# Decoder trunk: the first two unit pairs of each up projection go product by product, with their weights split during the projection before

## The chip, the core and the metric

One core of a Trainium2 chip runs the whole kernel. The metric is the device time in microseconds, as the median of several runs. PE is TensorE, DVE is VectorE, ACT is ScalarE, SP is the engine whose queue issues most DMAs.

## What is computed

The reference is a decoder trunk of two layers on x of 1024 tokens by 1024 features, float32. Layer 0 mixes by sparse attention beside a short gated convolution, layer 1 by a recurrent block (RG-LRU). Each layer ends with a gated convolution FFN, which is where the change lies:

```python
def rmsnorm(x, g):
    y = x * rsqrt(mean(x * x) + 1e-6)
    return y * g
def conv_ffn(h, w_up, conv_w, conv_b, w_down):
    u = causal_dwconv(h @ w_up, conv_w, conv_b)
    return (silu(u[..., :D_FF]) * u[..., D_FF:]) @ w_down
x = x + mixer(rmsnorm(x, norm_mix))
x = x + conv_ffn(rmsnorm(x, norm_ffn), ...)
```

D_FF is 2816, so `w_up` is 1024 by 5632 and `w_down` 2816 by 1024.

## The kernel before, in words

**Precision.** Every matmul of weights is made of three: operands are split into a high part (ACT copies the float32 to fp32r) and a low part (DVE subtracts the high part from the original), and `mm3` (L139) adds high by high, high by low, low by high. `split` (L145) is this pair of operations, so each weight tile and each activation tile costs one ACT and one DVE operation before PE may use it.

**The residual** X lies in SBUF as 8 feature chunks by 2 token halves, tiles of 128x512. While an FFN's up projection runs, X is in DRAM (`xd`): each finished half chunk is stored from ACT's queue (`ProductNorm.add`) and loaded again before the down projection.

**The up projection** (`up_pairs`, L312) uses a seven-product scheme for 2x2 blocks (Strassen in Winograd's form) in place of eight. Channels are taken in 22 pairs of units, a gate unit and an up unit of 128 channels each. A pair is seven products, named 1 to 7; a product is 12 matmuls of 128x512 into a PSUM bank. The left operands are halves of weight tiles or of their sums (`wA` for products 1 and 2, `w4` for 4, `sums` then `wG` for 6 and 3, `wU` for 7 and 5). The right operands are seven "pages" of four tiles each, high and low: the normalised X chunks and their differences. Pages 1 and 2 need the first token half alone. Page 5 needs scaled chunks of the second half, page 3 is the second half itself, 6 and 7 are differences, and 4 builds on 6. The banks: 1, 6, 7, 4 add up in bank A, 5 and 3 in bank Bk, 2 is in C; copies and additions between them (`c1`, `c2`, copies to `zu`, `zg`) yield the unit's z tiles, which `post` convolves (one ACT and two DVE operations of 1024 columns for each of two units), gates and stores to `fd` in DRAM.

**The order.** Everything in `up_pairs` is inside `in_order` (L95), which ties each instruction to the one before it on its engine, so PE, DVE, ACT and SP each run this stage in exactly the order of the text. Outside such a block a list scheduler orders each engine's instructions, with earlier program text first. The block begins

```python
wA(0), w4(0), sums(0), wG(0), wU(0), wA(1)
load(2)
p1(0), c1(0), p2(0), p1(1), c1(1), p2(1)
```

and then takes each pair as 5, 6, (1 of the next), 7, 3, (2 of the next), 4.

**The entry to an FFN.** `ProductNorm` collects the squares of X: ACT squares a chunk, DVE adds it to a running sum, and `rstd` multiplies by a matrix of ones on PE (`ss`, L1339, full float32), then ACT takes Ln and Exp to get R. For the first token half `done` does this and makes pages 1 and 2. For the second half `finish` (called at the start of `ffn`, outside the in-order block) does it and makes the pages 5, 6, 7, 3, 4 in turn, all before the block in program order. In layer 0 the entry is the end of `even_layer`: X's two halves are loaded from `yd`, the first half is squared and stored to `xd` again, and the rest of the attention's output projection (four tiles `W`, 24 matmuls each) is added to the second half. In layer 1 it is `down_last` (L269) of the recurrent block: four tiles `D` of 12 matmuls each and each token half, and `done` for the first half after the third tile of the second half.

**The turn to the down projection.** After the block the main pools are opened again, X is loaded, the y tiles (`yr` from `fd`, four channels for the first group) are split into pages, and `down` (L254) multiplies group by group into PSUM tiles `D` (four buffers of two banks), which `accum` adds to X.

Of the kernel before, what the change touches and what calls it, by code (L numbers as in the profile page):

```python
# [18 lines left out]
FP = mybir.dt.float32  # L19
# [40 lines left out]
class Kern:  # L60
# [60 lines left out]
    def split_w(self, raw, n=1024, pool_lo=False, parts=1):  # L121
        nc = self.nc
        self.nw += 1
        W, b = (self.W2, 1) if self.W2 is not None and self.nw % 3 == 0 else (self.W, 2)
        hi = W.tile([P, 1024], FR, tag="wh", bufs=b, name=self.nm("wh"))
        lo = W.tile([P, 1024], FR, tag="wl", bufs=b, name=self.nm("wl"))
# [5 lines left out]
        return hi, lo  # L132

# [120 lines left out]
    def down(self, wsrc, ng, ys, bias=None):  # L254
        nf = 8 // ng
        for ft in range(8 // nf):
            w = self.load_w(wsrc(ft))
# [11 lines left out]
    def down_last(self, wsrc, ng, ys, fin):  # L269
        nf = 8 // ng  # L270
        ws_ = [self.load_w(wsrc(ft)) for ft in range(8 // nf)]
        prev = None
        for sl in fin.slices:
# [4 lines left out]
            for f0 in range(0, 8, 2):  # L278
# [19 lines left out]
    def pages(self, p, xn):  # L298
        hi, lo = (self.page(p) for _ in range(2))
        return self.split(hi, lo, xn)  # L300

    def page(self, p):
        pool, bufs = (self.Bp, 24) if p in "374" else (self.Ap, 32)
        return pool.tile([P, HT], FR, tag="h", bufs=bufs, name=self.nm("h"))
# [7 lines left out]
    def up_pairs(self, srcs, B, post):  # L312

        nc = self.nc
        n = len(srcs)
        act, v = nc.scalar.activation, nc.vector.tensor_tensor
        raw, wt, st = {}, {}, {}
        at = lambda w, h: [x[:, half_of(h)] for x in w]  # L320
        bank = lambda: self.Q.tile([P, HT], FP, tag="q", bufs=8, name=self.nm("q"))
        z = lambda: self.cp.tile([P, S], FP, tag="c", bufs=6, name=self.nm("z"))

        def load(i):
            if i < n:
                raw[i] = [self.load_raw(srcs[i][0])]
                raw[i].append(self.W3.tile([P, S], FP, tag="wr", bufs=2, name=self.nm("wr")))
                nc.sync.dma_start(raw[i][1], srcs[i][1])

        def hi_lo(pool, n, tag, bufs, x):  # L330
            t = lambda c: pool.tile([P, n], FR, tag=tag + c, bufs=bufs, name=self.nm(tag + c))
            return self.split(t("h"), t("l"), x)
# [1162 lines left out]
```

## Time and profile before

| | us |
|---|---|
| runs: median (lowest, highest) | 2444.49 (2443.89, 2446.0) |
| the profiled execution | 2452.43 |
| its span, first to last instruction | 2449.8 |
| PE busy | 2275.6 (93%) |
| DVE busy | 1699.5 (69%) |
| ACT busy | 1166.2 (48%) |

Mean granted clock of TensorE: 0.961. All rows come from the one profiled execution; they are read as shares and differences, which are then set against the median of the runs. A row of the timeline gives the start, the length, the operation and in brackets the idle time of the engine before it with what ended it. Matmuls overlap, so the spacing of starts is what a matmul costs, not its length. `L141`, `L142` and `L143` are the three matmuls of `mm3`, so products are told apart by their operands (`q<-h,wh`: 1 and 2; `q<-h,sh`: 5, 6, 7, 3; `q<-h,ah`: 4).

### The profile page before, as it was taken

Reading aid. Unit: us, or ns where it says so; the run is one execution under the profiler, and the core shown is the slowest. Engines: PE = TensorE matmul, PEld = TensorE weight load, DVE = VectorE, ACT = ScalarE, POOL = GpSimd, SP = SyncE. Lnnn points to the kernel's source line nnn. Section 1 sums busy time; section 2 is a strip of 40 time slices with the busy share of each in tenths; the row PEclk is TensorE's granted clock in tenths of the full one; section 3 lists DMA queues with packets and bytes.
Section 4 is the critical chain, followed back from the end, with each engine's and each line's share of the span. In section 5 each row is a group of like instructions: output and inputs, shape, how many; then the busy total and the mean of one; then the engine's idle time right before and its main releaser. Section 6 shows DMA issues by size and latency. Waiting matters only on the chain.

```text
span 2449.8 us, 26485 instructions
## 1 busy us (share of the span) xinstructions
PE 2275.6 (93%) x10162; PEld 1842.5 (75%) x10162; DVE 1699.5 (69%) x2448; ACT 1166.2 (48%) x1699; POOL 170.2 (7%) x123
## 2 busy tenths in 40 slices
PE   7899999999659999999999999998599999999997
PEld 5788777777438888887888777886488888878886
DVE  6456778988687777777534657768787777765346
ACT  5652666766444444444212365575344444432114
POOL 4002233221000000000000210000000000000001
PEclk9899999999879999999999999999799999999998
DMA  4113112222421222222513111112122222243221
GB/s 140 57 54 117 52 52 69 91 78 83 159 86 69 78 89 92 78 78 101 208 52 104 45 48 56 44 49 103 35 78 78 81 95 83 73 176 129 78 78 69
DMA packets 71327, 207.27 MB, mean 85 GB/s; under 512 B 7969, under 2 KB 11553, under 8 KB 71073
## 3 DMA queue, kind: packets, MB, share of 16 engines
q1 hardware_dynamic: 65088, 193.79, 23.2%
q10 hardware_dynamic: 5472, 9.71, 1.0%
q0 software_dynamic: 640, 2.10, 0.2%
q8 instruction: 79, 1.29, 0.2%
q14 instruction: 48, 0.39, 0.0%
HBM read 161.52 MB, written 44.04 MB: 84 GB/s over the span
## 4 chain that ended last, share of the span: by engine, by line
PE 71%; DVE 10%; ACT 4%; issue 2%; DMA 1%; POOL 0%; DVEq 0%; ACTq 0%; SPq 0%; POOLq 0%
PE q L143 12%; PE q L141 11%; PE q L142 11%; PE D L142 7%; PE D L143 7%; PE D L141 7%; PE U L143 2%; PE U L142 2%; PE U L141 2%; PE T L939 2%; PE O L922 2%; DVE h L147 1%; PE F L141 1%; PE F L142 1%; PE F L143 1%
## 5 line engine op out<-in xcount | busy, mean ns | idle before, releaser
L130 ACT ACTIVATE wh<-wr 128x1024 fp32r<-128x1024 f32 x120 | 127.0, 1058 | 392.8 <-PE D L142 274.1
L141 PE MATMUL q<-h,sh 128*128 128x512 f32 x704 | 277.2, 394 | 2.7 <-ACT z L396 2.7
L142 PE MATMUL q<-h,sh 128*128 128x512 f32 x704 | 277.1, 394 | 0.0
L143 PE MATMUL q<-h,sl 128*128 128x512 f32 x704 | 277.1, 394 | 0.0
L250 DVE TENSOR_TENSOR x<-D,x 128x512 f32<-128x512 f32 x192 | 123.8, 685 | 205.7 <-PE D L143 203.9
L244 DVE SCALAR_TENSOR_TENSOR c<-z,par,c 128x1023 f32<-128x1023 f32 (+1 forms) x176 | 225.2, 1280 | 12.3 <-ACT c L242 9.2
L141 PE MATMUL U<-hh,wh 128*128 128x512 f32 x480 | 191.2, 399 | 12.7 <-ACT wh L130 12.7
L142 PE MATMUL U<-hl,wh 128*128 128x512 f32 x480 | 191.3, 399 | 7.2 <-DVE hl L195 7.1
L143 PE MATMUL U<-hh,wl 128*128 128x512 f32 x480 | 190.2, 397 | 2.2 <-DVE wl L131 2.2
L141 PE MATMUL q<-h,wh 128*128 128x512 f32 x352 | 143.3, 407 | 48.1 <-ACT wh L146 48.1
L141 PE MATMUL D<-y,wh 128*128 128x512 f32 (+1 forms) x464 | 180.9, 391 | 0.0
L143 PE MATMUL D<-y,wl 128*128 128x512 f32 (+1 forms) x464 | 180.8, 390 | 0.0
L142 PE MATMUL D<-y,wh 128*128 128x512 f32 (+1 forms) x464 | 180.8, 390 | 0.0
L141 PEld LDWEIGHTS q<-h,sh 128*128 128x128 f32 x704 | 132.2, 188 | 34.4 <-ACT z L396 4.4
L142 PEld LDWEIGHTS q<-h,sh 128*128 128x128 f32 x704 | 132.3, 188 | 30.5
L143 PEld LDWEIGHTS q<-h,sl 128*128 128x128 f32 x704 | 132.4, 188 | 30.3
L242 ACT ACTIVATE c<-z,par 128x1024 f32<-128x1024 f32 x88 | 109.2, 1240 | 89.8 <-DVE z L406 89.7
L143 PE MATMUL q<-h,wl 128*128 128x512 f32 x352 | 141.0, 401 | 2.6 <-DVE wl L147 2.6
L142 PE MATMUL q<-h,wh 128*128 128x512 f32 x352 | 140.5, 399 | 0.0
L131 DVE TENSOR_TENSOR wl<-wr,wh 128x1024 fp32r<-128x1024 f32 x96 | 120.5, 1257 | 26.7 <-ACT wh L130 23.5
L147 DVE TENSOR_TENSOR sl<-wr,sh 128x1024 fp32r<-128x1024 f32 x88 | 107.6, 1225 | 43.4 <-ACT sh L146 43.4
L146 ACT ACTIVATE sh<-wr 128x1024 fp32r<-128x1024 f32 x88 | 92.6, 1055 | 85.3 <-PE q L142 80.5
(310 smaller groups left out, 5292.7 us busy)
## 6 DMA issues: line engine op xcount, KB each, us to landing
wr<-in_wup SPq DMA_DIRECT2D x88, 512.0 KB, 4.3
fd<-c SPq DMA_DIRECT2D x44, 512.0 KB, 2.9
yr<-fd SPq DMA_DIRECT2D x44, 512.0 KB, 4.2
wr<-in_wd SPq DMA_DIRECT2D x40, 512.0 KB, 3.7
wr<-in_wbc SPq DMA_DIRECT2D x24, 512.0 KB, 3.5
xd<-x ACTq DMA_DIRECT2D x32, 256.0 KB, 2.1
x<-xd SPq DMA_DIRECT2D x32, 256.0 KB, 6.1
wr<-in_cin SPq DMA_DIRECT2D x16, 512.0 KB, 3.6
```

The lines of the kernel that those rows point to most:

```text
L130: nc.scalar.activation(hi[:, s], raw[:, s], AF.Copy)
L131: eng.tensor_tensor(lo[:, s], raw[:, s], hi[:, s].bitcast(FP), op=OP.subtract)
L141: mm(out, whi, xhi, start=first, stop=False, skip_group_check=resumed)
L142: mm(out, whi, xlo, start=False, stop=False, skip_group_check=resumed)
L143: mm(out, wlo, xhi, start=False, stop=last, skip_group_check=resumed)
L146: self.nc.scalar.activation(hi, t, AF.Copy)
L147: (eng or self.nc.vector).tensor_tensor(lo, t, hi.bitcast(FP), op=OP.subtract)
L242: nc.scalar.activation(o, src, AF.Identity, bias=b, scale=w(K - 1))
L244: nc.vector.scalar_tensor_tensor(o[:, s:], src[:, :n - s], w(K - 1 - s), o[:, s:], op0=OP.mult, op1=OP.add)
L250: nc.vector.tensor_tensor(x, ps, x, op=OP.add)
L922: nc.tensor.matmul(O, vv, hl[k], start=False, stop=last and k == 1)
L939: nc.tensor.transpose(T[:, hh * P:hh * P + P], cur["P"][:, hh, kb * P:kb * P + P], self.ident)
```

## The change

A class `Up` takes the place of `up_pairs`, with the order inside a steady pair the same but for `post`, whose first step moves behind the next pair's `w4` and whose last (the multiply and the store to `fd`) comes before `wA` of the next but one.

- **Weights early.** `fin.weights()` (`Up.prologue`) stands in `down_last` and in the attention's output projection after its second tile. It loads the weights of pairs 0 and 1, splits for both the halves of products 1, 2 and 4 (512 columns each) and makes the weight sums, in pools of their own.
- **Products as pages come.** `lead`, all of it in the in-order block, takes both pairs together: products 1, 2; page 5, products 5; page 3, products 3; page 6, products 6; page 7, products 7; page 4, products 4; the half weights of each product are split just behind its page. Product 1 of pair 2 follows, then the rest of the preparation for pairs 2 and 3 and the gating of pair 0.
- **The sums of squares** of the second half are no longer added on DVE: the eight squares are multiplied by ones on PE one by one into `ss` (eight matmuls of full float32 in place of one), six of them inside the projection. The first half keeps its sum on DVE; its `done` now comes after the first tile of the second half (layer 1, `late = 0`) or after the second W tile (layer 0), where two of the four W weights are loaded ahead and the first half of X isn't stored, since `yd` holds it.
- **Residual tiles turn into pages.** X's pool stays open with 16 rotating tiles; page 7, the low parts of page 4 and the tiles of `w4` take those whose values are used up.
- **The turn.** Before the last pair, inside the block, the first down weight and the first four y channels are loaded (through the two raw weight buffers) and split. X is loaded chunk by chunk, both halves.

```diff
@@ Kern
-    def down(self, wsrc, ng, ys, bias=None):
+    def down(self, wsrc, ng, ys, bias=None, pre=()):
...
-            w = self.load_w(wsrc(ft))
+            w = pre.pop(0) if pre else self.load_w(wsrc(ft))
...
     def down_last(self, wsrc, ng, ys, fin):
...
         ws_ = [self.load_w(wsrc(ft)) for ft in range(8 // nf)]
+        fin.weights()
...
-                if prev is not None and f0 == 4:
+                if prev is not None and f0 == fin.late:
...
     def ffn(self, l, nm, fin):
...
-            nm.finish()
-            self.main_close()
             self.us.close()
...
+            with self.pool(f"Q{l}", space=PS) as up.Q, self.in_order():
+                up.lead(nm, right)
+                up.steady()
+                cur = [up.y_pages(ci) for ci in range(UP_GROUPS[0][1])]
+                up.finish()
...
+        pre = [up.wd, self.load_w(io["wd"][l, 0, 1])]
+        for f in range(KC):
+            for half in range(2):
+                nc.sync.dma_start(self.X[f][half], self.xd[half][f][:, half_of(half)])
...
@@ even_layer
-        ws = [self.load_w(io["woa"][0, 0])]
+        ws = [self.load_w(io["woa"][0, ft]) for ft in range(2)]
...
-                    fin.add(f, 0, self.X[f][0])
-        fin.done(slice(0, HT))
+                    fin.add(f, 0, self.X[f][0], False)
...
+            if ft < 2:
+                ws.append(self.load_w(io["woa"][0, ft + 2]))
+            if ft == 1:
+                fin.weights()
...
+            if ft == 1:
+                fin.done(slice(0, HT))
...
+class Up:
+    RAW = {"1": (0, 0), "2": (0, 1), "6": (0, 0), "3": (0, 1), "7": (1, 0), "5": (1, 1)}
...
+    def half(self, p, i):
+        r, h = self.RAW[p]
+        self.wt[i, p] = self.hi_lo(self.Wx, HT, "x", 4, self.raw[i][r][:, half_of(h)])
...
+    def prologue(self):
+        k = self.k
+        self.pages()
+        self.Wx = self.xs.enter_context(k.pool(f"Wx{self.l}"))
+        for i in range(2):
+            self.load(i)
+        for p in "12":
+            for i in range(2):
+                self.half(p, i)
+        for i in range(2):
+            self.w4(i)
+        for i in range(2):
+            self.sums(i)
+
+    def lead(self, nm, right):
+        k, two = self.k, (0, 1)
+        nm.rstd1()
+        for i in two:
+            self.p1(i)
+        for i in two:
+            self.p2(i)
+        nm.page5()
+        for i in two:
+            self.half("5", i)
+        for i in two:
+            self.c1(i)
...
+        for i in two:
+            self.mm(i, "5", Bk[i], True)
+        nm.page3()
+        for i in two:
+            self.half("3", i)
+        for i in two:
+            self.act(zu[i][:, HT:], Bk[i])
+        for i in two:
+            self.mm(i, "3", Bk[i], False)
+        nm.page6()
+        for i in two:
+            self.half("6", i)
+        for i in two:
+            self.c2(i)
+        for i in two:
+            self.mm(i, "6", A[i], False)
+        nm.page7()
+        for i in two:
+            self.half("7", i)
+        for i in (2, 3):
+            self.load(i)
+        for i in two:
+            self.act(zg[i][:, HT:], A[i])
+        for i in two:
+            self.mm(i, "7", A[i], False)
+        nm.page4()
+        for i in two:
+            self.v(zg[i][:, HT:], Bk[i], zg[i][:, HT:], OP.add)
+        self.wA(2)
+        for i in two:
+            self.v(zu[i][:, HT:], A[i], zu[i][:, HT:], OP.add)
+        for i in two:
+            self.mm(i, "4", A[i], False)
+        self.p1(2)
...
+        self.w4(2)
+        self.sums(2)
+        self.act(zu[0][:, :HT], A[0])
+        self.wU(2)
+        t = self.post(0, (zg[0], zu[0]))
+        next(t)
+        self.act(zu[1][:, :HT], A[1])
+        self.c1(2)
+        self.p2(2)
+        self.wG(2)
+        self.wA(3)
...
+    def y_pages(self, ci):
+        k = self.k
+        if ci == 0:
+            self.wd = k.load_w(k.io["wd"][self.l, 0, 0])
+        raw = k.load_raw(k.fd[ci])
+        return k.y_halves(raw)
+
+    def finish(self):
+        self.pair(self.n - 1)
+        for _ in self.tail:
+            pass
...
 class ProductNorm:
...
+    late = 0
...
+            t = self.up.sq[f]
+            nc.scalar.activation(t, x, AF.Square)
+            self.t.append(t)
+            if f % 2 and f > 1:
+                self.sums(f - 3)
...
+    def sums(self, f0):
...
+        for f in (f0, f0 + 1):
+            nc.tensor.matmul(self.ss, k.ones, self.t[f], start=f == 0, stop=f == KC - 1)
...
+    def rstd1(self):
+        self.k.ln_exp(self.R[:, HT:], self.ss)
...
+    def page5(self):
+        k, X = self.k, self.k.X
+        self.up.B["5"] = [(k.page(), k.page()) for _ in range(4)]
         for i in range(4):
-            b11, b12 = X[i][0], self.scaled(i, 1)
-            v(b11, b12, b11, op=OP.subtract)
-            B["5"][i] = k.pages("5", b11)
+            self.minus(X[i][0], self.scaled(i, 1), X[i][0])
+            k.split(*self.up.B["5"][i], X[i][0])
...
+    def page7(self):
+        k, X = self.k, self.k.X
         for i in range(4):
-            B["3"][i] = k.pages("3", X[4 + i][1])
-        for i in range(4):
-            b21, t2 = X[4 + i][0], X[i][0]
-            v(b21, b21, t2, op=OP.subtract)
-            B["4"][i] = k.pages("4", b21)
+            self.minus(X[i][1], X[4 + i][1], X[i][1])
+        hi, lo = ([k.x_tile(FR) for _ in range(4)] for _ in range(2))
+        self.up.B["7"] = [k.split(hi[i], lo[i], X[i][1]) for i in range(4)]
```

## Rows read from the trace of the kernel before

**Rows 1.** The page, part 1: busy us, share, instructions.

```profile
PE 2275.6 (93%) x10162; PEld 1842.5 (75%) x10162; DVE 1699.5 (69%) x2448; ACT 1166.2 (48%) x1699; POOL 170.2 (7%) x123
```

**Rows 2.** Waits of PE: us in total, times, longest.

```profile
PE q L141 <- ACT wh L146: 48.1, 2, 25.2
PE ss L1339 <- DVE sq L210: 34.3, 3, 20.1
PE D L141 <- ACT h L146: 7.4, 2, 3.7
PE q L141 <- ACT z L396: 2.7, 4, 0.7
PE D L142 <- DVE h L147: 1.5, 2, 0.8
```

**Rows 3.** Windows: length, busy by engine (PE, PEld, DVE, ACT, POOL), clock, DMA.

```profile
690.00:736.00 46.00, 18.44 (x52) 13.11 (x52) 36.93 (x57) 19.34 (x31) 0.00 (x0) 0.63 0.11 36
...
789.30:1137.18 347.88, 347.88 (x1513) 284.08 (x1512) 273.54 (x289) 166.78 (x199) 0.00 (x0) 1.00 0.23 81
1812.69:2160.57 347.88, 347.88 (x1514) 284.06 (x1512) 273.56 (x289) 166.79 (x199) 0.00 (x0) 1.00 0.23 81
```

**Rows 4.** Timeline of PE, layer 0: start, us, operation, idle before.

```profile
662.76 2.08 PE L1339 MATMUL ss<-sq,ones 128*128 128x512 f32 x2 [20.08 <-DVE sq L210]
...
689.79 0.39 PE L143 MATMUL W<-og,wl 128*128 128x512 f32 x1
693.21 2.07 PE L1339 MATMUL ss<-sq,ones 128*128 128x512 f32 x2 [3.03 <-DVE sq L210]
...
725.59 0.79 PE L141 MATMUL q<-h,wh 128*128 128x512 f32 x1 [22.92 <-ACT wh L146]
...
735.88 0.39 PE L141 MATMUL q<-h,sh 128*128 128x512 f32 x1
```

**Rows 5.** The same of layer 1.

```profile
1700.02 1.02 PE L1339 MATMUL ss<-sq,ones 128*128 128x512 f32 x2
...
1703.41 0.39 PE L143 MATMUL D<-g,wl 128*128 128x512 f32 x1
...
1714.98 2.07 PE L1339 MATMUL ss<-sq,ones 128*128 128x512 f32 x2 [11.19 <-DVE sq L210]
...
1759.26 0.39 PE L141 MATMUL q<-h,sh 128*128 128x512 f32 x1
```

**Rows 6.** Groups of DVE, 1684 to 1760: busy us, mean ns, idle before.

```profile
L147 DVE TENSOR_TENSOR h<-x,h 128x512 fp32r<-128x512 f32 x28 | 18.8, 681 | 0.0
L1346 DVE SCALAR_TENSOR_TENSOR x<-x,par,R 128x512 f32<-128x512 f32 x16 | 11.5, 744 | 0.0
L289 DVE TENSOR_TENSOR x<-D,x 128x512 f32<-128x512 f32 x16 | 10.3, 685 | 3.2 <-PE D L143 3.0
L210 DVE TENSOR_TENSOR sq<-sq,sq 128x512 f32<-128x512 f32 x14 | 9.6, 686 | 0.8 <-ACT sq L206 0.2
...
L345 DVE TENSOR_TENSOR wr<-wr 128x512 f32<-128x512 f32 x1 | 0.7, 683 | 0.0
```

**Rows 7.** One group of ACT over the run; four page lows running on DVE.

```profile
L146 ACT ACTIVATE h<-x 128x512 fp32r<-128x512 f32 x56 | 33.1, 624 | 28.0 <-DVE x L1355 10.8 <-DVE x L1359 9.9 <-DVE x L1363 3.5
...
722.47 2.49 DVE L147 TENSOR_TENSOR h<-x,h 128x512 fp32r<-128x512 f32 x4
```

**Rows 8.** Timeline of PE at the turn to down, layer 0.

```profile
1155.86 0.73 PE L141 MATMUL D<-h,wh 128*128 128x512 f32 x2 [3.69 <-ACT h L146]
...
1157.95 0.63 PE L143 MATMUL D<-h,wl 128*128 128x512 f32 x1
...
1163.61 0.39 PE L142 MATMUL D<-h,wh 128*128 128x512 f32 x1
```

**Rows 9.** The page, part 6: DMA issues, count, KB each, us to landing.

```profile
yr<-fd SPq DMA_DIRECT2D x44, 512.0 KB, 4.2
```

**Rows 10.** Timeline of SP's queue, layer 0.

```profile
645.30 14.47 SPq L1175 DMA_DIRECT2D x<-yd  x16
```

More of the change, by code (lines that the diff above doesn't have):

```diff
@@ L296, in down_last @@
         fin.done(prev)
[L298 to L304, printed above, removed]
     def product(self, out, w, pages, first):
@@ L454, in ys @@
                     if g < 2:
-                        hl = [self.pages("1", raw[:, half_of(h)]) for h in range(2)]
-                        out.append([[hl[h][k] for h in range(2)] for k in range(2)])
+                        out.append(self.y_halves(raw))
                     else:
@@ L467, in ffn, with page, y_halves @@
                     nxt = ys(g + 1)
-                    self.down(lambda ft: io["wd"][l, g, ft], n, cur)
-                    cur = nxt
+                    self.down(lambda ft: io["wd"][l, g, ft], n, cur, None, pre)
+                    cur, pre = nxt, ()
+    def page(self, dt=FR):
+        return self.Ap.tile([P, HT], dt, tag="h", bufs=32, name=self.nm("h"))
+    def y_halves(self, raw):
+        hl = [self.split(self.page(), self.page(), raw[:, half_of(h)]) for h in range(2)]
+        return [[hl[h][k] for h in range(2)] for k in range(2)]
     def open_U(self):
@@ L1303, with weights @@
     slices = [slice(0, HT), slice(HT, S)]
+    late = 4
     def __init__(self, k, gi):
         self.k, self.nm = k, k.new_norm(gi)
+    def weights(self):
+        pass
     def add(self, f, half, x):
@@ L1315, with __init__, weights @@
 class ProductNorm:
     slices = [slice(0, HT), slice(HT, S)]
-    def __init__(self, k, gi):
+    late = 0
+    def __init__(self, k, gi, l):
         self.k, self.nm = k, self
         self.st = k.new_norm(gi)
-        self.B = {p: [None] * 4 for p in "1234567"}
-    def add(self, f, half, x):
-        k = self.k
-        k.sq_add(self.st, half, x, k.nc.vector)
-        k.nc.scalar.dma_start(k.xd[f][:, half_of(half)], x)
+        self.up = Up(k, l)
+        self.t = []
+    def weights(self):
+        self.up.prologue()
@@ new lines, in add @@
+    def add(self, f, half, x, spill=True):
+        k, nc = self.k, self.k.nc
+        if half == 0:
+            k.sq_add(self.st, 0, x, nc.vector)
+        else:
+            self.up.pages()
+            t = self.up.sq[f]
[3 more added lines that the diff above has]
+                self.sums(f - 3)
+        if spill:
+            if half == 0:
+                k.xd = [k.xd[1], k.xd[1]]
+            nc.scalar.dma_start(k.xd[half][f][:, half_of(half)], x)
@@ L1332, in done @@
             for c in range(KC):
-                p = "12"[c // 4]
-                self.B[p][c % 4] = self.k.pages(p, self.scaled(c, 0))
-    def rstd(self, h):
-        k, nc = self.k, self.k.nc
-        ss = k.newU("ss")[:, :HT]
-        nc.tensor.matmul(ss, k.ones, self.st["acc"][h], start=True, stop=True)
-        if h == 0:
-            self.R = k.Rp.tile([P, S], FP, tag="R", bufs=1, name=k.nm("R"))
-        k.ln_exp(self.R[:, half_of(h)], ss, h == 0)
+                k.split(*self.up.B["12"[c // 4]][c % 4], self.scaled(c, 0))
+        else:
+            self.sums(KC - 2)
@@ L1375, with weights @@
     pool_part = [(0, 2, 4, 6), (0, 2, 4), (1, 4)]
+    late = 4
+    def weights(self):
+        pass
     def __init__(self, k):
```

337 lines of the change are left out of this document (193 added, 144 removed).

## The prediction

> **What bounds the kernel now.** I read the page's busy shares first, then what TensorE (PE) waits for, then the windows and timelines of the places where it waits. PE is busy 93% of the span, VectorE (DVE) 69%, ScalarE (ACT) 48% [rows 1]. So only PE's idle time and its slow-clock time can be won. The list of PE's waits [rows 2] is short where the diff works: 48.1 us in two waits before a product of the up projection, 34.3 us in three waits before the sum of squares `ss`, 8.9 us before the first down matmuls, 2.7 us in four waits on a `z` copy.
>
> The steady part has nothing to give: pairs 3 to 20 of each layer take 347.88 us with PE busy for all of it at granted clock 1.00 [rows 3], 19.33 us a pair, 2.76 us a product of 12 matmuls, 0.230 us a matmul. The loss lies at the entries. Layer 0: PE sits from 642 to 662.76 waiting for `ss`; the projection ends at 689.8, `ss` runs at 693.21, products 1 and 2 of pair 0 follow, and then PE waits 22.92 us until 725.59; pair 0's product 5 starts at 735.88 [rows 4]. In 690 to 736 PE is busy 18.44 of 46 us at a mean clock of 0.63 [rows 3]. Layer 1 is alike: last D matmul 1703.41, 11.19 us wait for `ss`, product 5 of pair 0 at 1759.26 [rows 5]. The releaser named, ACT `wh`, had no work of its own: it is wA(1), which the hand-written order puts after the weight sums of pair 0, and DVE does those only among and behind the page splits. The third place is the turn from up to down [rows 8].
>
> I compare times at the end of pair 2, from where both orders run alike: 789.30 and 1812.69 before [rows 3].
>
> **The lead, part by part.** In the new order three DVE stretches follow each other: (a) what must be done until the second half's R is there and DVE is free, at a time I call D0; (b) DVE's list in `lead`; (c) PE's remainder.
>
> (a) Layer 0. DVE starts when X's first half is in. Its loads are 16 issues from 645.30 over 14.47 us [rows 10]; the old sum ended at 662.7 with the spill DMAs in ACT's queue, which for this half are dropped; I take 660. After it: 8 accumulations at 0.64, 2 weight lows at 1.2, 8 scalings at 0.66 and 8 page lows at 0.60, then the prologue: 6 half-weight lows at 0.60 and 8 weight sums at 0.7 [rows 6, 7]. That is 5.1 + 2.4 + 10.1 + 3.6 + 5.6 = 26.8, so 687; with 2 us of idle, D0 = 689. The first two W units now run before `ss`, so PE's 20 us wait goes, but DVE's list is longer than PE's W work and decides. Layer 1. The last D phase is 96 matmuls, 22 us, ending at 1703.6, so its first accumulation is due at 1684.7. DVE then has 16 accumulations 10.3, half of the 14 square additions 4.8, pages 1 and 2 10.1, two lows and eight sums 6.8: 32 us, to 1717; D0 = 1718. The other condition, R, is earlier: 1703.6, plus six ones-matmuls at 1.02 inside the phase [rows 5], last accumulations 1.3, square 0.6, two more ones-matmuls 2.0, two ACT operations of 0.62 to 0.7 [rows 7], is 1715. So the 7 additional ones-matmuls (7.1 us of PE per entry) cost nothing under DVE's list; if DVE were faster they would show. Bounds of D0: 683 to 699 and 1713 to 1727, the late ends if the prologue runs before the accumulations and R's chain of 5 us is left with DVE idle.
>
> (b) `lead` is inside the in-order block, page operations too, so DVE waits at each page for ACT's high part, which it didn't before. Page 5: scaling 0.66, difference 0.68, ACT high 0.62 [rows 7], low 0.60 and hand-overs: 2.7 each, 10.8. Page 3: 2.0 each, 8.0. Page 6: two differences and a low, 8.0 with hand-overs. Page 7: 4.8. Page 4: 2.4. Eight half-weight lows: 4.8. Additions c2 and zg: 2.6. wA(2): 1.2. First zu addition: 0.6. Sum 43.2. Once more DVE waits: page 4's high part stands on ACT behind the copy of product 6 of pair 1, 2.6. So product 4 of pair 0 can start at D0 + 46.
>
> (c) From there to the end of pair 2 PE has 11 products (4, 4, 1, 2, and pair 2's seven): 30.4. Pair 2's product 7 waits for an ACT copy that stands behind pair 1's first convolution (it frees the z buffer): 2.6, and about 2 of slow clock. End of pair 2: D0 + 81, that is 770 and 1799. **Gain: 19 and 14.** PE's gaps in the lead before that (some 4, 1, 3.5 and 1.6 us before products 5, 3, 6, 4) are in DVE's chain and count once.
>
> **Steady part: nothing.** DVE works 273.5 us in 18 pairs of 347.88 [rows 3], so 4.1 us a pair are left; the multiply of the gate moves one product ahead, the SP queue keeps store, then loads. If that cover fails, each 0.1 us a pair costs 3.8 us over both layers.
>
> **The turn to down.** Before: a 0.69 wait in pair 21, 3.7 and 0.8 before the first D matmuls, and a slow clock from 1155.86 to about 1163.5, where a matmul takes 0.63 for 0.39 [rows 2, 8]: about 8.3 us lost in layer 0, 7.2 in layer 1. After: these go, but `y_pages` for four channels stands in the in-order block before pair 21, so on ACT behind the last copy of pair 20 and ahead of pair 21's copies. Their raw tiles share two buffers with the down weight: channel 1 loads only after the weight is split, channel 2 after channel 0, channel 3 after channel 1. A load takes 4.2 us from issue to landing [rows 9]. Counted from the end of pair 20: weight split done 2.9, channel 1 lands 7.4, is split 9.2, channel 3 lands 13.6, is split on ACT 14.9, a convolution and two copies follow: product 7 starts at 17.8, where products 5 and 6 ended at 5.5. PE stands 12.3 us and then about 17 matmuls are slow, 3.4: 15.7 lost per layer, net **minus 7.4 and minus 8.5**. Queued behind it on SP is only the store of channel 20, which nobody needs for four groups; the reload of X is covered by four PSUM tiles of 5.5 us. Bounds: no wait at all (plus 16 over both layers) to minus 24.
>
> **Sum:** 19 + 14 - 16 = 17 us. The profiled execution took 2452.43 us around a span of 2449.8; the median of the runs is 2444.49, 0.3% lower, and I subtract from that: **2427 us**.
>
> **A rule weighed against the trace.** After waits of 3.0 and 22.9 us PE's next matmuls ran slow, granted 0.63 in that stretch; after 0.69 us in the steady part the window's clock reads 1.00 [rows 3, 4]. So I charge slow matmuls after the long gaps only. The Trainium skill, "TensorE: Matmul & The Clock Gate", section "HAM oscillation", says that bursts of matmuls parted by idle gaps can each start at half clock again, which speaks against a lead of short bursts; by it the lead would be the second rival below. No row shows which holds for gaps of 1 to 4 us in series.
>
> **The rivals.**
> 1. The last pair isn't held up (the loads are covered, or the copies come first). For it: DMA engines are busy only 23% there [rows 3]. Against: two buffers and one ACT order. Then no 15.7 is lost: 17 + 31 = 48, minus what the first down group loses in their place, some 7: about 2403. Chance 0.15.
> 2. Slower: the clock stays at its lower level (1.2 of 2.4 GHz) through the interleaved products. From product 5 to product 4 of the first two pairs are 10 products; slow, each costs 12 x 0.24 = 2.9, 29 us, of which the gaps take up 7 and 5 are charged already: 17 an entry, 34 in all, so 17 us slower: 2461. It turns to slower once some 35 more matmuls an entry are slow. For it: 0.63 in the old lead. Against: that stretch was 60% idle, this one is some 15% idle. Chance 0.10.
> 3. D0 is late: the prologue's fourteen DVE operations run before the accumulations, so R comes last and DVE idles on it. 6 to 8 us an entry, gain about 3: 2441. For it: the prologue stands earlier in the program. Against: its weights land late. Chance 0.18.
> 4. DVE's list is shorter than I count (D0 at the early ends): 11 more, 2416. Chance 0.10.
>
> **How the numbers follow.** My case has 0.47. A measurement of this kernel tells about 0.2% from no change, 4.9 us. My case spreads by its bounds from 2410 to 2444, so a little of it falls within 0.2%. Faster: 0.44 + 0.15 + 0.10 and a part of rival 3, 0.73; same 0.16; slower 0.11. The range 2402 to 2447 holds my case and rivals 1, 3 and 4 and leaves out rival 2 and tails.
>
> **What would show it.** Right: PE idle over 20 us gone at both entries; DVE nearly without gaps from about 660 to the end of the lead, with some 0.8 us before each low of pages 5 and 3; end of pair 2 81 us after DVE starts page 5; a wait of 10 to 13 us before product 7 of pair 21 released by an ACT copy, none before the first D. Wrong: PE gaps in the lead released by PE's own clock, pairs longer than 19.33 us, or pair 21 without its wait.

## The result, and the profile after

The changed kernel takes 2418.8 us (median of 4 runs, 2410.37 to 2420.19); the kernel before, run beside it, 2445.24. The ratio is 0.988, 95% interval 0.9853 to 0.9908: a gain clear of the noise, though under 2%, of 26 us on the medians (22 to 36 by the interval) where 17 were forecast. The two profiled executions differ by more, 41.2 us in span: attention alone, which the change doesn't touch, ended 8.9 us earlier in the profile after (granted clock up to there 0.98, and 0.95 before). So time is compared below stretch by stretch, each from a mark that both programs pass.

The page after, part 1, answers to [rows 1]:

```profile
PE 2280.0 (95%) x10190; PEld 1833.6 (76%) x10190; DVE 1679.2 (70%) x2446; ACT 1159.7 (48%) x1710; POOL 170.6 (7%) x123
```

PE is busy 95% of a shorter span. Its waits after, where the diff works (they answer to [rows 2]):

```profile
PE q L146 <- ACT z L1229: 31.3, 6, 11.1
...
PE ss L1502 <- ACT h L1488: 8.0, 3, 6.6
...
PE ss L1508 <- DVE sq L215: 6.1, 1, 6.1
...
PE q L146 <- ACT xh L151: 3.7, 4, 1.5
```

The 48.1 us before two products are gone, and of the 34.3 before `ss` 14.1 are left. The wait for `z` copies has grown from 2.7 us to 31.3; 20.5 of it are two waits at the turn. Windows after: the lead of layer 0 by the same clock times as in [rows 3], and pairs 3 to 20 of both layers (length, busy by engine, clock, DMA):

```profile
690.00:736.00 46.00, 38.76 (x157) 29.74 (x156) 42.90 (x74) 25.39 (x39) 0.00 (x0) 0.96 0.19 69
750.36:1101.11 350.75, 350.75 (x1513) 283.81 (x1512) 269.47 (x296) 162.71 (x197) 0.00 (x0) 1.00 0.23 81
1763.78:2114.53 350.75, 350.75 (x1513) 283.81 (x1512) 269.14 (x289) 162.65 (x197) 0.00 (x0) 1.00 0.23 81
```

Two things to see: the stretch where PE was busy 18.44 of 46 us at clock 0.63 now has 38.76 at 0.96 (counted from the last F matmul, which came 8.9 us earlier, the same 46 us have 37.15 at 0.96); and pairs 3 to 20, 347.88 us before, take 2.87 more, with PE busy all the time and the clock at 1.00. PE's timeline through the first entry (answers to [rows 4]):

```profile
651.64 3.78 PE L1502 MATMUL ss<-h,ones 128*128 128x512 f32 x4 [6.60 <-ACT h L1488]
...
687.10 0.50 PE L146 MATMUL q<-h,xh 128*128 128x512 f32 x1 [1.54 <-ACT xh L151]
...
697.52 0.79 PE L146 MATMUL q<-h,xh 128*128 128x512 f32 x1 [4.33 <-ACT z L1229]
...
719.75 0.47 PE L146 MATMUL q<-h,ah 128*128 128x512 f32 x1 [0.73 <-DVE z L1232]
```

No gap is over 6.6 us where gaps of 20 and 22.9 stood; 719.75 is product 4 of pair 0. In layer 1 the longest is the 6.11 us before `ss` in the list above, for the 11.19 of [rows 5]. DVE at the first scaling of the second half, layer 0:

```profile
670.39 1.88 DVE L255 TENSOR_TENSOR x<-W,x 128x512 f32<-128x512 f32 x3
676.06 0.75 DVE L1521 SCALAR_TENSOR_TENSOR x<-x,par,R 128x512 f32<-128x512 f32 x1 [3.79 <-ACT R L224]
```

676.06 is what the forecast calls D0. DVE had finished its list and waited 3.79 us for R. The same in layer 1, with the end of the weight sums and the first accumulations ahead:

```profile
1648.70 2.49 DVE L152 TENSOR_TENSOR xl<-wr,xh 128x512 fp32r<-128x512 f32 x4
...
1656.44 1.28 DVE L1232 TENSOR_TENSOR wr<-wr 128x512 f32<-128x512 f32 x2
1657.64 3.07 DVE L296 TENSOR_TENSOR x<-D,x 128x512 f32<-128x512 f32 x5
...
1671.66 2.08 DVE L1521 SCALAR_TENSOR_TENSOR x<-x,par,R 128x512 f32<-128x512 f32 x3 [3.55 <-ACT R L224]
...
1689.50 0.75 DVE L1521 SCALAR_TENSOR_TENSOR x<-x,par,R 128x512 f32<-128x512 f32 x1 [4.04 <-ACT R L224]
```

The turn in layer 0: PE at pair 21's product 7, then ACT in the same time:

```profile
1116.28 0.79 PE L146 MATMUL q<-x,sh 128*128 128x512 f32 x1 [9.40 <-ACT z L1229]
```

```profile
1103.65 1.16 ACT L151 ACTIVATE h<-wr 128x512 fp32r<-128x512 f32 x2 [0.31 <-DMA wr<-fd]
1107.71 1.15 ACT L151 ACTIVATE h<-wr 128x512 fp32r<-128x512 f32 x2 [2.90 <-DMA wr<-fd]
1110.30 1.15 ACT L151 ACTIVATE h<-wr 128x512 fp32r<-128x512 f32 x2 [1.45 <-DMA wr<-fd]
1112.98 1.15 ACT L151 ACTIVATE h<-wr 128x512 fp32r<-128x512 f32 x2 [1.53 <-DMA wr<-fd]
1114.03 1.23 ACT L247 ACTIVATE o<-z,par 128x1024 f32<-128x1024 f32 x1
1115.16 1.06 ACT L1229 ACTIVATE z<-q 128x512 f32<-128x512 f32 x2
```

The four `h<-wr` rows are the y channels, each waiting for its load; the copies that free pair 21 (`z<-q`) come at 1115.16. In place of [rows 8] the first D matmul then follows with no wait.

Where the 41.2 us between the two profiles came from, from the first matmul of each stretch (the mark for the last 96 out-projection matmuls lies two matmuls, 0.45 us, ahead of them in every run; the tail begins at the sum of squares of the last norm):

| stretch | before | after | gain | forecast |
|---|---|---|---|---|
| start to the last F matmul | 642.29 | 633.41 | 8.9 | - |
| to pair 3, layer 0 | 147.01 | 116.95 | 30.1 | 19 |
| pairs 3 to 20 | 347.88 | 350.75 | -2.9 | 0 |
| pair 21 and down | 267.16 | 269.85 | -2.7 | -7.4 |
| to the last 96 out-projection matmuls | 276.01 | 274.73 | 1.3 | 0 |
| to pair 3, layer 1 | 132.34 | 118.09 | 14.3 | 14 |
| pairs 3 to 20 | 347.88 | 350.75 | -2.9 | 0 |
| pair 21 to the last norm | 276.86 | 282.83 | -6.0 | -8.5 |
| tail | 12.37 | 11.24 | 1.1 | 0 |

### The profile page after: what moved, and what is told of

The parts are those of the page before. It is cut to its first block, busy times and chain, and to the rows that moved or that the text cites. A ratio compares the mean times of both kernels' runs of the same rounds, so it can differ in the third digit from the quotient of the medians.

```text
span 2408.6 us, 26588 instructions
## 1 busy us (share of the span) xinstructions
PE 2280.0 (95%) x10190; PEld 1833.6 (76%) x10190; DVE 1679.2 (70%) x2446; ACT 1159.7 (48%) x1710; POOL 170.6 (7%) x123
## 4 chain that ended last, share of the span: by engine, by line
PE 68%; DVE 11%; ACT 5%; issue 2%; DMA 2%; POOL 0%; SPq 0%; DVEq 0%; ACTq 0%; POOLq 0%
PE q L146 11%; PE q L147 11%; PE q L148 11%; PE D L146 7%; PE D L147 7%; PE D L148 7%; PE U L147 2%; PE U L146 2%; PE U L148 2%; PE O L814 2%; PE T L831 2%; PE F L146 1%; PE F L147 1%; PE F L148 1%; DVE h L152 1%
## 5 line engine op out<-in xcount | busy, mean ns | idle before, releaser
L1229 ACT ACTIVATE z<-q 128x512 f32<-128x512 f32 x176 | 103.5, 594 | 371.0 <-PE q L148 370.8
L249 DVE SCALAR_TENSOR_TENSOR o<-z,par,o 128x1023 f32<-128x1023 f32 (+1 forms) x176 | 225.4, 1282 | 26.1 <-ACT o L247 23.1
L146 PE MATMUL q<-h,sh 128*128 128x512 f32 x480 | 189.9, 396 | 0.0
L148 PE MATMUL q<-h,sl 128*128 128x512 f32 x480 | 189.1, 394 | 0.0
L147 PE MATMUL q<-h,sh 128*128 128x512 f32 x480 | 188.8, 393 | 0.0
L147 PE MATMUL q<-h,wh 128*128 128x512 f32 x320 | 125.9, 393 | 0.0
L146 PE MATMUL q<-h,wh 128*128 128x512 f32 x320 | 124.9, 390 | 0.0
L791 ACT ACTIVATE P<-P,m 128x640 f32<-128x640 f32 (+7 forms) x128 | 93.5, 730 | 46.3 <-DVE m L789 45.9
L247 ACT ACTIVATE o<-z,par 128x1024 f32<-128x1024 f32 x88 | 108.7, 1235 | 7.2 <-DMA fd<-o 4.6
L1232 DVE TENSOR_TENSOR z<-q,z 128x512 f32<-128x512 f32 x132 | 90.0, 686 | 30.8 <-PE q L148 30.8
L152 DVE TENSOR_TENSOR pl<-T,ph 128x512 fp32r<-128x512 f32 x132 | 89.2, 686 | 28.6 <-ACT ph L151 27.2
L148 PEld LDWEIGHTS q<-h,sl 128*128 128x128 f32 x480 | 90.2, 188 | 21.9
```

What stands on the lines that cost most here:

```text
L146: mm(out, whi, xhi, start=first, stop=False, skip_group_check=resumed)
L147: mm(out, whi, xlo, start=False, stop=False, skip_group_check=resumed)
L148: mm(out, wlo, xhi, start=False, stop=last, skip_group_check=resumed)
L152: (eng or self.nc.vector).tensor_tensor(lo, t, hi.bitcast(FP), op=OP.subtract)
L247: nc.scalar.activation(o, src, AF.Identity, bias=b, scale=w(K - 1))
L249: nc.vector.scalar_tensor_tensor(o[:, s:], src[:, :n - s], w(K - 1 - s), o[:, s:], op0=OP.mult, op1=OP.add)
```

## The experiments

All times are medians; "ratio" is against the kernel before in the same set of runs (the changed kernel's is 0.988). "Entry" is the time from the last F matmul, or from the mark at the last 96 out-projection matmuls, to pair 3: 116.95 and 118.09 in the changed kernel.

**Is interleaving needed?** The lead with all pages first:

```diff
         nm.page5()
+        nm.page3()
+        nm.page6()
+        nm.page7()
+        nm.page4()
         for i in two:
             self.half("5", i)
...
-        nm.page3()
         for i in two:
             self.half("3", i)
...
```

> The changed kernel with the lead's product order undone: all pages (5, 3, 6, 7, 4) are made right behind products 1 and 2, and only then come the weight halves and products 5, 3, 6, 7, 4 of the two pairs; the early weight halves, the sums of the projection and the steady part stay. Theory (interleaving hides the products under VectorE's list): VectorE needs about 34 us for the pages, then ten products of 2.78 us with their halves follow one after another, so product 4 of the second pair ends some 64 us behind the start of page 5 in place of 48: 13 to 16 us lost at each entry, about 2447, no better than before. Rival (the gain came from the weights split during the projection and from the sums on PE, since VectorE's list is the bound with either order): at most 4 us an entry, 2419 to 2427.

Measured: 2451.43 us, ratio 1.0006 (0.9993 to 1.0019). The net gain is gone. The entries are 133.15 and 132.48, that is 16.2 and 14.4 longer, and PE waits once in each, for the halves that now stand behind all pages, about as long as it did before:

```profile
PE q L146 <- ACT xh L151: 46.2, 2, 23.6
```

In layer 1 that is the entry of the kernel before (132.34). In layer 0 it is still 10.6 to 13.9 us shorter than before (143.78 and 147.01 in the two profiles with the old entry); the longer pairs and the turn use that up.

**Early weights.** The splits and sums of the prologue moved to the head of `lead`, whose start moves up ahead of them; the loads stay where they were:

```diff
         for i in range(2):
             self.load(i)
+
+    def lead(self, nm, right):
+        k, two = self.k, (0, 1)
+        nm.rstd1()
         for p in "12":
             for i in range(2):
...
         for i in range(2):
             self.sums(i)
-
-    def lead(self, nm, right):
-        k, two = self.k, (0, 1)
-        nm.rstd1()
         for i in two:
             self.p1(i)
```

> The changed kernel with the six weight halves and eight weight sums of the first two pairs not in the projection but at the head of the lead, behind the second half's R; the loads stay early. Theory: VectorE has 6 x 0.60 + 8 x 0.70 = 9.2 us more between R and page 5, and ScalarE's six halves come first; products 1 and 2 and page 5 start 8 to 9 us later, and what VectorE saves ahead of R brings R at most 1 us earlier, so 7 to 9 us lost at each entry: about 2435. Rival (VectorE's list ahead of R sets R, as the forecast had it for both layers: D0 moves earlier by the same 9 us): 0 to 2 us an entry, 2419 to 2423.

Measured: 2432.64 us, ratio 0.9937 (0.9914 to 0.9960); entries 123.85 and 125.13, so 6.9 and 7.0 longer. The rival falls: with 9.2 us less on VectorE's list ahead of it, the second half's R comes only 2.8 and 2.7 us earlier behind the mark (39.84 for 42.62, 41.10 for 43.77), and the moved work then stands between R and page 5. R in layer 1, in the changed kernel and here (the marks are 1645.69 and 1654.28):

```profile
1688.83 0.63 ACT L224 ACTIVATE R<-R 128x512 f32<-128x512 f32 x1
```

```profile
1694.75 0.63 ACT L224 ACTIVATE R<-R 128x512 f32<-128x512 f32 x1
```

**The order in layer 0.** `done` of the first half before the W units (the pools of the pages are opened there too, which isn't shown):

```diff
@@ even_layer
+        fin.done(slice(0, HT))
         OA = self.OA
...
-            if ft == 1:
-                fin.done(slice(0, HT))
...
```

> The changed kernel with the first half's norm finished before the out projection of layer 0, as it was before, and not between its second and third unit. Only layer 0 is touched. Theory (VectorE's list decides when the second half's R is there, PE has slack): PE waits some 20 us for the first sum again, but VectorE can start scaling only when that sum is there in either order; the projection then runs behind, R comes later by the two units that no longer run in that wait (5.6 us) less the idle time that PE has today before the last units: 3 to 6 us lost, about 2423. Rival (the wait of 20 us before the sum was the loss): 15 to 20 us lost, about 2437.

Measured: 2428.53 us, ratio 0.9914 (0.9895 to 0.9934). The entry of layer 0 is 127.31, 10.4 longer, between the two; that of layer 1 stays at 117.73. PE waits 15.1 us for the first half's sum again (the other 6.1 of this row are layer 1's, as before the edit):

```profile
PE ss L1508 <- DVE sq L215: 21.2, 2, 15.1
```

The entry grows by less than that, since the changed kernel waits 6.6 us there too, for the second half's squares. DVE is hit as well: it then waits 5.4 us for the first W unit.

**The sums on PE.** The second half's squares added on DVE, one matmul with the ones:

```diff
@@ ProductNorm.add
-            t = self.up.sq[f]
-            nc.scalar.activation(t, x, AF.Square)
-            self.t.append(t)
-            if f % 2 and f > 1:
-                self.sums(f - 3)
+            k.sq_add(self.st, 1, x, nc.vector)
...
```

> The changed kernel with the squares of the second half summed on VectorE again (seven additions an entry) and one matmul with the ones, as before, in place of eight matmuls. Theory (VectorE's list and R's chain are nearly equal: the trace shows VectorE idle 3.8 us before the second half's first scaling): the additions take 7 x 0.69 = 4.8 us of VectorE, 3.8 of it in that idle time, and lengthen R's chain by one addition less one matmul of 0.9; the second half's R comes 1 to 3 us later at each entry: 2421 to 2425. Rival (the eight matmuls at 0.85 to 1.0 us are on the path, since R was last in both layers): 1 to 4 us an entry are gained, 2411 to 2417.

Measured: 2430.54 us, ratio 0.9925 (0.9908 to 0.9942); entries 124.95 and 121.08. Layer 1 loses 3.0, as expected; layer 0 loses 8.0, so the time is above the 2421 to 2425 expected. There DVE adds the last squares only behind the pages 1 and 2, and PE waits for the sum:

```profile
PE ss L1511 <- DVE sq L215: 15.1, 1, 15.1
```

**The turn.** Loads at the end of pair 20 into four raw buffers in place of two, splits behind the copies of pair 21 (the two comments are added here):

```diff
@@ Up.pair
         self.act(zg[:, HT:], A)
         self.step()
+        self.y_w(i)          # down weight, load of channel 3
+        self.y(i, 0)
...
         self.v(zu[:, HT:], A, zu[:, HT:], OP.add)
+        self.y(i, 1)
...
         self.v(zg[:, HT:], Bk, zg[:, HT:], OP.add)
+        self.y(i, 2)
...
         self.load(i + 3)
+        if i == self.n - 2:
+            self.y_load()    # wd, fd[0] in "wr"; fd[1], fd[2] in "wv"
...
         self.act(zu[:, :HT], A)
+        self.y(i, 3)
...
```

> The changed kernel with another turn from up to down: the first down weight and the four y channels are loaded at the end of pair 20 into four raw buffers (the two of the W pool and the two of the wv pool, only the fourth channel waits for the split weight), and their splits stand behind the copies of pair 21, one after another between its products. Theory (pair 21 is held up because the y splits stand before its copies on ScalarE): the waits of 9.40 and 11.10 us before product 7 fall below 1.5 us, the slow matmuls behind them go too (about 2 us each), the first D group waits less than 2 us: 18 to 24 us less, about 2398. Rival (the loads can't come sooner; the wait only moves): the first D matmuls wait 6 us or more in each layer, at most 8 us less, 2411 or more.

Measured: 2396.09 us, ratio 0.9793 (0.9764 to 0.9821). From pair 21's first matmul to the first of down it is 16.04 us in both layers, against 25.48 and 28.14 in the changed kernel and 18.7 before. PE's waits in that stretch of layer 0:

```profile
PE q L146 <- DVE z L1232: 0.9, 1, 0.9
PE q L146 <- ACT z L1229: 0.7, 1, 0.7
```

**The longer pairs.** The clock is 1.00 and PE has no gap, so the matmuls themselves come slower: 0.2320 us apart on the mean, 0.2301 before. By product the spacing lies between two speeds, 0.2267 and some 0.234. Before, products 6 and 1 had 0.2267 and products 7 and 3 0.234; after, no product has 0.2267 throughout. The change moved the pool W4 (weight halves of products 5, 6, 7, 3) from 110-134 to 164-188 thousand bytes of a partition, by the compiled kernels' lists of tiles, and to addresses at odd multiples of 32. Three runs with an empty tile ahead of what lies on the right side (in the kernel before not in the recurrent block); shortened:

```diff
@@ ffn, rglru, the down projection
+            self.right_pad(right)   # [P, 8] float32: 32 bytes; [P, 16] in the control
```

> The changed kernel with one empty tile of 32 bytes per partition at the start of the right-hand side of SBUF in both feed-forward layers, in the recurrent layer and in the down projections; nothing else. Theory (placement by offset): in the two traces matmuls come every 0.2267 us where both operands begin at a multiple of 64 bytes and every 0.234 us where one begins at an odd multiple of 32, and the change moved the weight halves of products 5, 6, 7 and 3 to such places. Then pairs 3 to 20 take 342.8 us a layer (0.2267 a matmul) instead of 350.75, the y groups of the down projections (1392 matmuls, 0.0075 each) 10 us less and the out projection of the recurrent layer 3 us less: 32 us in all, about 2387. Rival 1 (region: the upper part of SBUF is slower, whatever the offset): no change, 350.75 a layer, 2419. Rival 2 (VectorE's and ScalarE's traffic beside the matmuls): no change either.

> The control to the run before: the same empty tile, but of 64 bytes, so that everything on the right-hand side moves by 64 and keeps its offset. Theory (placement by offset): no change, pairs 3 to 20 take 350.75 us a layer within 0.3. Rival (any shift of the tiles changes something, or the run-to-run spread is taken for an effect): as much as the 32-byte tile.

> The kernel before with the same 32-byte tile. Theory (placement by offset): pairs 3 to 20 take 342.8 us a layer instead of 347.88, the y groups 10 us less, the out projection of the recurrent layer as before (its tiles were well placed): about 12 + 10 = 22 us less, about 2423. So with both kernels padded the steady part is equal, and the change as such is worth some 36 us, not 26. Rival (the change's longer pairs come from its other order in the pair or from more work on VectorE beside PE): the padded kernel before keeps 347.88.

Measured: 2414.64 us, ratio 0.9861 (0.9842 to 0.9881); the control 2419.66 in one run; the padded kernel before 2440.74, ratio 0.9968 (0.9951 to 0.9984). The window of pairs 3 to 20 in layer 0, in that order:

```profile
762.00:1110.12 348.12, 348.12 (x1514) 284.33 (x1513) 269.54 (x296) 162.41 (x197) 0.00 (x0) 1.00 0.24 81
```

```profile
761.23:1111.03 349.80, 349.80 (x1514) 284.20 (x1512) 269.50 (x296) 162.56 (x197) 0.00 (x0) 1.00 0.24 81
```

```profile
786.27:1132.35 346.08, 346.08 (x1514) 283.94 (x1513) 273.62 (x289) 166.80 (x199) 0.00 (x0) 1.00 0.24 81
```

The 32 bytes give a third of what was expected of them in this window: 2.6 us instead of 7.9 (and 2415 and 2441 us for the 2387 and 2423 expected), and the control, expected at zero, moved by 0.95. With both kernels padded the changed one's pairs are still 2.0 us longer. Products 6 and 7, at even multiples of 32 now, kept 0.233. So the region was tried, with W4 on the left and the tiles of the convolutions in its stead:

```diff
@@ Up.lead
-        self.op = self.xs.enter_context(k.pool(f"o{self.l}"))
-        self.W4 = right.enter_context(k.pool(f"W4{self.l}", side="right"))
+        self.W4 = self.xs.enter_context(k.pool(f"W4{self.l}"))
+        self.op = right.enter_context(k.pool(f"o{self.l}", side="right"))
```

> The changed kernel with the pool W4 (weight halves of products 5, 6, 7, 3) on the left side of SBUF, at 151 to 175 KB of a partition and at multiples of 64 bytes, in place of 164 to 188 KB on the right; the tiles of the convolutions go to the right in exchange. After the padded runs, where the 32-byte offset gave only a part of the expected. Theory (region with offset: a matmul is slow, 0.2333, when an operand lies in the uppermost part, and the change moved these weights there): products 5, 6, 1 and 7 come at 0.2267 a matmul again, 3 stays at 0.234 by its pages, pairs 3 to 20 take 345.4 us a layer instead of 350.75, 13 us less over all pairs, about 2406. Rival (the longer pairs come from VectorE's other order beside PE, or from the pages' places): pairs stay at 349 to 351, 2416 to 2419.

Measured: 2412.04 us, ratio 0.9847 (0.9826 to 0.9868), and

```profile
763.35:1109.55 346.20, 346.20 (x1514) 283.96 (x1512) 267.72 (x289) 162.55 (x197) 0.00 (x0) 1.00 0.24 82
```

346.20 for the 345.4 expected; the median came out at 2412 for 2406. Products 6, 1 and 7 are at 0.2267 and product 5 at 0.229. The region isn't the reason, though: product 3, both of whose operands lie in the uppermost part in the changed kernel, had 0.2302 there and goes to 0.2338 now that its weights lie lower. And product 1 gained (0.2314 to 0.2267) with its own operands where they were. In the timeline, the first matmuls of product 6 and of the product behind it, in the changed kernel and with W4 on the left:

```profile
753.15 0.40 PE L146 MATMUL q<-h,sh 128*128 128x512 f32 x1
...
755.95 0.40 PE L146 MATMUL q<-h,wh 128*128 128x512 f32 x1
```

```profile
766.10 0.39 PE L146 MATMUL q<-h,sh 128*128 128x512 f32 x1
...
768.82 0.39 PE L146 MATMUL q<-h,wh 128*128 128x512 f32 x1
```

2.80 us for twelve matmuls against 2.72. No single matmul row shows the difference; the distance of their starts does. The rival, VectorE's other order, can't be the reason: it is the same in both. The last section has a pattern that fits all these products.

**Together.** The turn, W4 on the left and the padding in one kernel; then also down groups 2 and 3 from low pages (`if g < 4` for `if g < 2` in `ffn`):

> The three edits that showed a gain together: the new turn, W4 on the left, and the 32-byte tile for what stays on the right. Theory (they work in different stretches and on TensorE alone, so they add): the turn 22 us, W4 4.55 us for 18 pairs a layer, so 10 us over all, the offset of the pages of products 3 and 4 and of the y tiles some 4 us: 36 us under the changed kernel, 2383 (2378 to 2390); pairs 3 to 20 take 345 us a layer, no wait over 2 us in pair 21 or before the first down matmul. Rival (VectorE, 83% busy in a pair of 19.49 us, becomes the bound in a pair of 19.2, or the new turn loses its slack when PE is faster): PE waits appear in the pairs or at the first down matmul, 2392 or more.

> The combined kernel, with the hidden tiles of down groups 2 and 3 also split into the pages of the A pool (44 to 116 KB of a partition) in place of the y pool at 180 to 221 KB. Theory (region): their 768 matmuls over both layers come at 0.2267 in place of 0.2333 to 0.234, 5 us less than the combined kernel. Rival (two splits of 512 columns in place of one of 1024 for each channel make ScalarE and VectorE later, or the pages come free late): no gain or PE waits before the groups, 0 to 5 us more.

Measured: 2381.67 us, ratio 0.9724 (0.9701 to 0.9747), and 2377.12 us, ratio 0.9695 (0.9675 to 0.9715). Pairs 3 to 20 take 345.48 us in both, pair 21 to down 15.9, with no wait over 0.9 us, so the rival's waits didn't come. Between the first and the last down matmul the second saves 2.8 us in layer 0 and 1.7 in layer 1. Both beat the changed kernel, the second by 1.9% of the time.

**The start of page 5 in layer 1.** `late = 6` for `late = 0` in `ProductNorm`, on top of the last kernel:

> The combined kernel with the A pool's pages, and at the entry of layer 1 the first half's sum, R and pages 1 and 2 behind the fourth pair of units of the second half, not behind the first (late = 6 for 0). In the changed kernel the weight splits run ahead of the first accumulations there (1648.70 to 1657.64), PE waits 6.11 us for the first half's sum, and pages 1 and 2 (1671.66 to 1682.37) stand ahead of six of the second half's accumulations, whose R starts product page 5 at 1689.50. Theory (this order, not the amount of VectorE's work, made the start of page 5 in layer 1 six microseconds later than the forecast had it): PE's 6.11 us wait goes, the second half's R is ready before pages 1 and 2 are, and page 5 starts 4 to 7 us earlier; from the first of the last 96 matmuls of the out projection to the end of pair 2 it is 112 to 114 us in place of 118, 2372. Rival (VectorE's list is the bound, the idle 3.55 and 4.04 us only move behind the pages): 117 to 119, 2377.

Measured: 2386.64 us, ratio 0.9748 (0.9734 to 0.9761), and an entry of 121.82 us, longer than the 118.2 it had. The theory falls, and the rival's figure is passed too. DVE, with no page work to put between accumulations, waits for the matmuls and then for R; the second half's R comes 38.03 us behind the mark, 5.2 earlier than in the kernel that this one is built on (43.26), but pages 1 and 2 now stand between it and page 5:

```profile
DVE x L299 <- PE D L151: 7.7, 2, 4.5
DVE x L1547 <- ACT R L227: 4.2, 1, 4.2
```

```profile
1676.35 1.14 ACT L227 ACTIVATE R<-R 128x512 f32<-128x512 f32 x2
```

Of the 10.0 us between the two profiled spans 3.6 lie in this entry and 4.6 in attention, which is the same in both kernels.

## Why the prediction was right

The sign, the places and the mechanism held; the sum was 17 us for 26: layer 0's entry and the turn came out better than counted, the steady pairs worse.

**(a) D0.** In layer 0 the forecast had DVE's list as the last condition, 46.7 us behind the last F matmul. It came 42.65 behind it (676.06 less 633.41), and R, not the list, was last: 3.79 us of idle DVE. The list itself ended at 672.27, 38.9 behind the mark, so it was counted too long; four of the prologue's fourteen operations ran ahead of the squares already (631.19 to 635.1). This is what the fourth rival described, 4.1 us of it. In layer 1 D0 was 37.7 us behind the mark by the forecast and 43.8 by the trace, 6.2 late. Its mechanism is partly that of the third rival: the prologue's fourteen operations run from 1648.70, before all sixteen accumulations of the last 96 matmuls, and DVE idles 3.55 and 4.04 us on R; PE also waits 6.11 us for the first half's sum, which the forecast didn't have. With the prologue moved behind R that R came 2.7 us earlier, with the first half's sum and pages moved to the end 5.2; neither shortened the entry, since page 5 then waited for the moved work (it started 50.8 and 46.5 us behind the mark). The step that the additional ones-matmuls cost nothing under DVE's list failed: R was last in both layers, and in layer 1 six of the eight ran behind the projection, where the forecast and the description of the change had six inside it:

```profile
1682.35 5.72 PE L1502 MATMUL ss<-h,ones 128*128 128x512 f32 x12 [0.50 <-ACT h L1488]
```

They are still the better way: adding on DVE instead lost 3.0 and 8.0 us.

**(b), (c) The lead and PE's remainder.** 46 and 35 us by the forecast. Product 4 starts 43.7 us behind D0 (719.75), and pair 3 30.6 us later, in both layers. (b) was 2.3 too long, (c) 4.4: the wait of 2.6 at pair 2's product 7 and the 2 us of slow clock didn't occur. The waits of DVE came as counted (0.70 for 0.8 us before the lows of pages 5 and 3). So layer 0 won 11 more than forecast (4.1 + 2.3 + 4.4), and layer 1's 14.3 for 14 is a hit by two errors of opposite sign, 6.2 late and 6.7 short. The 30.1 is also a good draw: eight of the runs share this entry's order, at 116.9 to 120.4 us, and two have the one before, at 143.8 and 147.0; the typical gain is 27.

**Steady part: "nothing".** Wrong by 2.87 us a layer, 5.7 together; pairs longer than 19.33 us, 19.49 here, are one of the signs of being wrong that the forecast named. The cover held, as said (no PE wait), but the step looked only at what could stall PE, and took the time of a matmul for fixed. Where the operands lie changed it; moving W4 to the left gave 4.55 us a layer.

**The turn.** The mechanism is as predicted, in place and releaser: 9.40 and 11.10 us at product 7 of pair 21 for 12.3, and no wait at the first D. The loads came somewhat sooner than counted: behind the end of pair 20 (1101.11), channel 1 was there at 6.6 us for 7.4 and channel 3 at 11.9 for 13.6. Net it cost 2.7 and 6.0 for 7.4 and 8.5. The first rival, which expected no wait here, is what the new turn then made true: 16.04 us from pair 21 to down.

**The second rival,** TensorE at its lower level through the interleaved products, is refuted for this lead: five gaps of 0.7 to 4.3 us between products, and a granted clock of 0.96 in 690 to 736. Under the rule of the Trainium skill's "TensorE: Matmul & The Clock Gate", section "HAM oscillation", each burst could have started slow; of the five bursts behind gaps in layer 0 one did. Behind the 4.33 us gap seven matmuls came 0.40 to 0.59 us apart at granted clock 0.50, and layer 1 has the same behind 4.30 us; behind the gaps of 0.7 to 1.5 us the clock stayed at its upper level:

```profile
697.17:700.59 3.42, 3.07 (x7) 2.48 (x8) 3.35 (x7) 1.51 (x4) 0.00 (x0) 0.50 0.00 0
700.60:736.00 35.40, 32.49 (x136) 24.96 (x135) 34.46 (x61) 20.75 (x31) 0.00 (x0) 1.00 0.25 90
```

(The forecast's own example for a short gap, 0.69 us, lies in pair 21, outside the window that it read; the clock there was 1.00 as well, from 1137.18 to 1155.86.)

What is the gain made of? With pages first the net gain is gone (30.8 us by the ratios); weights late cost 13.9, the old order in layer 0 8.3. They overlap, so they don't add up to 26. In layer 1 the interleaving is the condition for the whole gain. In layer 0 the 10.6 to 13.9 us that stay without it are about what the order of `done` and the W units is worth there (10.4).

## What to carry to other kernels

When an engine prepares operands in a list that another engine consumes, hand out the work in the order of consumption: the consumer's time then lies under the producer's, and only the last piece shows. Check what such a move puts ahead of the copies that free the consumer's buffers at the other end; here it put waits of 9.4 and 11.1 us there, and placing the same splits behind those copies, with two more raw buffers and earlier loads, won some 22 us (the order alone wasn't tried). And compare the spacing of like matmuls before and after, not only the gaps: tiles moved to other places cost 5.7 us with no wait in any list, and moving one pool gave 9.1 back.

## What the runs showed of the hardware that was not expected

At granted clock 1.00 a 512-column matmul comes every 0.2267 or every 0.232 to 0.235 us, by where its operands lie. In the out projection of the recurrent layer the moving operand `g` went from 155-180 to 205-229 thousand bytes of a partition, and the spacing from 0.2267 to 0.2342; in down groups with pages at 44-118 it is 0.2267, in those with y tiles at 180-221 it is 0.234; the weights of products 6 and 7, moved from 164-186 to 151-173, brought 0.2333 back to 0.2267. It is no simple bound on an address: weights at 219-227 thousand bytes ran at 0.2267 in the recurrent layer before.

One pattern in the compiled kernels' addresses fits all of this. Take the distance between the start of the moving operand and the start of the weights, and how many bytes it is off a multiple of 512. In the pairs 3 to 20 of layer 0, products in the order in which they run (bytes off: us a matmul):

| product | before | changed | W4 on the left |
|---|---|---|---|
| 5 | 0: 0.2306 | 160: 0.2328 | 0: 0.2291 |
| 6 | 0: 0.2267 | 160: 0.2332 | 0: 0.2267 |
| 1 of the next | 0: 0.2267 | 0: 0.2314 | 0: 0.2267 |
| 7 | 160: 0.2338 | 160: 0.2333 | 0: 0.2267 |
| 3 | 160: 0.2342 | 0: 0.2302 | 160: 0.2338 |
| 2 of the next | 0: 0.2283 | 0: 0.2306 | 0: 0.2278 |
| 4 | 0: 0.2302 | 0 and 160: 0.2323 | 0 and 160: 0.2320 |

At 0 the matmuls settle at 0.2267. Right behind a slow product they first come slower and reach 0.2267 only after some matmuls, the last two or three of the twelve in products 1, 3 and 2 of the changed kernel; that gives the values in between. So product 1 is slow behind a slow product 6, with its own operands unmoved. The out projection is at 0 before and at 160 after, down groups are at 0 with pages and at 160 with y tiles. The empty tile of 32 bytes made 128 of the 160, that of 64 bytes 96, neither of them 0, and they gave 2.6 and 0.95 us in 1512 matmuls. The pattern was found afterwards and no run was built to test it; a tile that brings the right side to 0 would. What in the chip makes it so is open.
